# Gate operands in pairs of two tokens, and a low half that is kept unscaled

## The chip, the cores and the metric

The kernel runs on one core of a Trainium2 chip. The metric is the device time of one execution in microseconds. The engines are named as in the profile: PE (TensorE's matmuls), PEld (TensorE's weight loads), DVE (VectorE), ACT (ScalarE), POOL (GpSimd) and SP (SyncE, which issues the weight DMAs).

## The reference

A decoder trunk of two layers on 256 tokens with 1024 features. Each layer has a token-mixing part (a recurrent group, a state-space group and windowed attention behind one input and one output projection), a normalisation, and a retrieval part (PEER), which is the one that matters here:

```
q = (x @ wq)  ->  8 heads, two halves;  scores against 2 x 128 keys
top 16 of each half, top 16 of their sums  ->  16 expert pairs (i, j) per head
gate = softmax(best 16)
act  = gelu(x . u[i*128 + j]);   out = sum gate * act * v[i*128 + j]
```

So each token uses 8 x 16 = 128 of the 128 x 128 experts, with a gate for each.

## The kernel before, in words

The retrieval doesn't gather. It computes the activation of all 16384 experts for all 256 tokens (the first product), multiplies by a dense gate matrix that is zero but at the chosen experts, and multiplies the result by all rows of v (the second product).

*First product* (L987 to L993). 128 steps per layer, one per block of 128 experts. A weight block of 128 x 1024 f32 (512 KB) comes by DMA from SP into `raw`. It is split into a high part `hi` (ACT, L117) and a low part `lo` = raw - hi (L118; on DVE, and for every third block from the fourth to the 109th on POOL). 24 matmuls of 256 columns follow: hi with the high part of x, hi with its low part, and lo with the high part. After two steps `uevac` (L973 to L981) applies the gelu on ACT. Where the gates of a token are there already it multiplies by them (DVE, L978).

*Gates.* `routing` (L852 to L928) finds the chosen experts of 128 tokens: top-16 searches on DVE, one-hot work and matmuls against an identity in bf16 (L918, 16 matmuls in a row). It leaves, for every token, the two key indices of its 128 choices in `ijT` and the gates in `gT`, choices along the partitions. `gT` holds a high half float (scaled by GS = 2^15) and the rest as a second half float (scaled by LS = 2^11 more). `wgen` (L961 to L971) then goes through the 64 groups of four tokens in three stages: `gates` makes the operands on DVE, `wmm` the matmuls on PE, `apply` puts the result into `act`.

For a group, `gates` (L933 to L943) compares the indices with 0 to 127 (`eq`, L937: one-hot rows of both halves), multiplies the first one-hot by the two halves of the gate (`ga`, parts 0 and 1, L940), and makes a copy of the second one-hot divided by LS (`ga`, part 2, L942), which takes the low half's scale out again. All three have the four tokens innermost:

```
eq = pool.tile([128, 2, 128, TG], F16, name="eq", bufs=2)
A = pool.tile([128, 3, 128, TG], F16, name="ga", bufs=2)
```

`wmm` (L945 to L950) contracts over the 128 choices, for each token two matmuls of 128 x 128 x 128: high half with one-hot, low half with scaled one-hot. Both operands of a token are read with a step of four half floats. `apply` (L952 to L960) multiplies by 1 / GS into `act`: on DVE for the c experts whose activation is there (L956), on ACT as a plain copy for the others (L958). As the steps go on c grows, and so do L956 and L978.

*Order.* `wgen` is background work: one stage is issued per step of the first product, behind the routing of both token blocks. The instruction order on each engine is planned ahead of time from estimated costs and priorities, so an engine may do work ahead of its place in the source; each engine then runs its own list in order.

*Second product* (L995 to L1037). The two first pairs of `act` are split into the places of `eq` and `ga` (`early`, L997).

Of the kernel before, what the change touches and what calls it, by code (L numbers as in the profile page):

```python
# [8 lines left out]
F32R = mybir.dt.float32r  # L9
BF16 = mybir.dt.bfloat16  # L10
F16 = mybir.dt.float16
U32 = mybir.dt.uint32
AF = mybir.ActivationFunctionType
OP = mybir.AluOpType
AX = mybir.AxisListType

D = 1024
SEQ = 256
# [28 lines left out]
def trunk(ctx, tc, x, wst, ut, vr, pp_d, rb_d, lnrow, bd_d, keys_d, out):  # L47
    nc = tc.nc
    PE, ACT, DVE, POOL, SP = nc.tensor, nc.scalar, nc.vector, nc.gpsimd, nc.sync

    const = ctx.enter_context(tc.tile_pool(name="const", bufs=1))
    hpool = ctx.enter_context(tc.tile_pool(name="hpool", bufs=1))
    stream = ctx.enter_context(tc.tile_pool(name="stream", bufs=1))
    psum = ctx.enter_context(tc.tile_pool(name="psum", bufs=1, space=bass.MemoryType.PSUM))
    dram = ctx.enter_context(tc.tile_pool(name="dram", bufs=1, space=bass.MemoryType.DRAM))

# [1 line left out]
    items = []  # L58
    index = {}

# [79 lines left out]
        pump_dma()  # L140


# [1 line left out]
    mixp = tc.tile_pool(name="mix0", bufs=1)  # L144
    mix = mixp.__enter__()
    jp = mix.tile([128, 128], F32, name="jp")
    POOL.iota(jp, pattern=[[1, 128]], base=0, channel_multiplier=-1, allow_small_or_imprecise_dtypes=True)
    ident = const.tile([128, 128], F32, name="ident")
    POOL.tensor_scalar(ident, jp, 0.0, None, op0=OP.is_equal)
    iota4 = const.tile([128, 128, 4], F16, name="iota4")  # L150
    iota16 = const.tile([128, 16, 16], BF16, name="iota16")
    identb = const.tile([128, 128], BF16, name="identb")
    tri_le = const.tile([128, 128], F32, name="tri_le")
# [14 lines left out]
        return rb[:, l, o:o + w]  # L168

    def make_consts():  # L170
        POOL.iota(iota4, pattern=[[1, 128], [0, 4]], base=0, channel_multiplier=0, allow_small_or_imprecise_dtypes=True)
        POOL.iota(iota16, pattern=[[1, 16], [0, 16]], base=0, channel_multiplier=0, allow_small_or_imprecise_dtypes=True)
        POOL.tensor_scalar(identb, jp, 0.0, None, op0=OP.is_equal)
        POOL.tensor_scalar(tri_le, jp, 0.0, None, op0=OP.is_ge)
        POOL.tensor_scalar(tri_gt, jp, 0.0, None, op0=OP.is_lt)
        POOL.tensor_scalar(tri_gr, jp, 0.0, None, op0=OP.is_lt)
        for i in range(4):
            POOL.tensor_scalar(mask0[:, i, :], jp, 0.0, NEG, op0=OP.is_gt, op1=OP.mult)
        for i in range(2):
            POOL.tensor_scalar(mask1[:, i, 0, :], jp, 0.0, NEG, op0=OP.is_le, op1=OP.mult)  # L180
            POOL.tensor_scalar(mask1[:, i, 1, :], jp, 0.0, NEG, op0=OP.is_gt, op1=OP.mult)
# [10 lines left out]
    def mm(ps, lhsT, rhs, start, stop):  # L192
        PE.matmul(ps, lhsT, rhs, start=start, stop=stop)  # L193
# [4 lines left out]
    def acc_bank():  # L198
        return psum.tile([128, 512], F32, name="acc", bufs=4)

# [1 line left out]
    def layer_norm(h, pool, pre, gb, store, nxt=None, final=False, after=None):  # L202
        """h [128, 2, D] in place, stored to store; returns the transposed split operands."""
        ring = isinstance(gb[0], tuple)
        g, b = (rawtile(k) for k in gb) if ring else gb
        with tc.high_priority():
            hT = layer_norm_(h, pool, pre, g, b, store, nxt and index[nxt], final, after)
        for k in gb if ring else ():
            rawdone(k)
        return hT  # L210
# [93 lines left out]
    def seq(t):  # L304
        return [(w[0],) + tuple(int(ch) for ch in w[1:]) for w in t.split()]

    # (step, token block, part): r residual and sums, m mean and squares, v variance, n reciprocal root, s centre and
    # gain, o scale and bias with the transposes, l low halves, p the next weight pieces
    LN_ORDER = (
        seq("r00 r01 m0 v0 s00 s01 n00 r10 n01 r11 n02 m1 n03 v1 o00 o01 s10 n10 s11 n11 l00 n12 p1 n13 o10 o11 l01 l10 l11 p2"),  # L310
        seq("r00 r01 m0 s00 s01 v0 r10 n00 r11 n01 m1 n02 n03 o00 v1 o01 s10 n10 s11 n11 n12 n13 p1 o10 o11 l00 l01 l10 l11 p2"),
        seq("r00 r01 m0 s00 s01 v0 n00 n01 n02 r10 n03 r11 m1 s10 s11 v1 o00 n10 o01 n11 n12 n13 o10 o11"))

# [1 line left out]
    class Background:  # L315
        def __init__(self):
            self.q = []
# [39 lines left out]
        return y  # L357

    def log1p_exp_neg_abs(pool, o, xin, n, tag):
        """o = max(x, 0) + log1p(exp(-|x|)) on [128, n]"""  # L360
        a = pool.tile([128, n], F32, name=tag + "_a")
        e = pool.tile([128, n], F32, name=tag + "_e")
        q = pool.tile([128, n], F32, name=tag + "_q")
        ACT.activation(a, xin, AF.Abs)
        ACT.activation(e, a, AF.Exp, scale=-1.0)
        DVE.tensor_scalar(a, e, 2.0, None, op0=OP.add)
        DVE.reciprocal(a, a)
        DVE.tensor_tensor(e, e, a, op=OP.mult)
        DVE.tensor_tensor(a, e, e, op=OP.mult)
        DVE.tensor_scalar(q, a, 1.0 / 17.0, None, op0=OP.mult)  # L370
        for c in (15, 13, 11, 9, 7, 5, 3):
            DVE.scalar_tensor_tensor(q, q, 1.0 / c, a, op0=OP.add, op1=OP.mult)
        DVE.scalar_tensor_tensor(q, q, 1.0, e, op0=OP.add, op1=OP.mult)
        DVE.tensor_scalar(o, xin, 0.0, None, op0=OP.max)
        DVE.scalar_tensor_tensor(o, q, 2.0, o, op0=OP.mult, op1=OP.add)

# [1 line left out]
    def layer_consts(l, mix):  # L378
        av = mix.tile([128, 16], F32, name="av")
        sp4 = mix.tile([128, 4], F32, name="sp4")  # L380
# [12 lines left out]
    def mixer(l, mix, h, hT, pre):  # L393
# [3 lines left out]
        yTl = mix.tile([128, 16, SEQ], F32R, name="yTl")  # L397
        xs = mix.tile([128, N_XBC, SEQ], F32, name="xs")

        # small per-layer values  # L400
        dt = mix.tile([128, 2, 16], F32, name="dt")
        da = mix.tile([128, 2, 16], F32, name="da")
        das = mix.tile([128, 2, 2, 16], F32R, name="das")
# [25 lines left out]
            yield  # L429
            yield  # L430

        # causal depthwise convolution
        def conv(o, xp, w0, bias=None):
            if bias is None:
                DVE.tensor_scalar(o, xp[:, 0:SEQ], w0(0), None, op0=OP.mult)
# [287 lines left out]
                stages[st_](*units[u])  # L723
                yield

        # projection schedule
        order = [8, 9, 10, 11, 0, 1, 2, 3, 4, 5, 6, 7]
        for n, blk in enumerate(order):
            ps = bank([128, SEQ])
# [5 lines left out]
            if n == 3:  # L735
                ps = bank([128, SEQ])
# [8 lines left out]
        for blk in range(4):  # L745
            ps = bank([128, SEQ])
# [6 lines left out]
        for blk in range(4):  # L753
            ps = bank([128, SEQ])
# [5 lines left out]
        for i in range(6):  # L760
            ps = bank([128, SEQ])
# [7 lines left out]
        for nh in range(2):  # L769
            pz = [acc_bank() for _ in range(2)]  # L770
            for kp in range(4):
                hi, lo = weights(("w", l, n0 + nh * 4 + kp))
                for kk in range(2):
                    k = kp * 2 + kk
# [9 lines left out]
                ACT.activation(sz[:, tb, nh * 512:(nh + 1) * 512], pz[tb], AF.Silu)  # L784
        n0 += N_Z
        bg.add(ssm_final())
        # output projection
        po = [[acc_bank() for _ in range(2)] for _ in range(2)]
        oorder = list(range(0, 16))
        def out_mm(i, kb, w, tb):  # L790
# [26 lines left out]

    RA, RB2, RX = 2, 2, 1

# [1 line left out]
    def peer(l, pool, hT):  # L821
        hTh, hTl = hT
        act = pool.tile([128, 128, SEQ], F32, name="act")
        ijT = pool.tile([128, 2, SEQ], F16, name="ijT")
        gT = pool.tile([128, 2, SEQ], F16, name="gT")

        def view(slot, n):
            return act[:, slot:slot + n, :].rearrange("p a b -> p (a b)")
# [23 lines left out]
        def routing(tb):  # L852
            base = 92
# [48 lines left out]
            DVE.reciprocal(sm[:, 8:16], sm[:, 0:8])  # L902
            DVE.tensor_tensor(ex, ex, sm[:, 8:16, None].to_broadcast([128, 8, 16]), op=OP.mult)
            yield
            ts = slice(tb * 128, (tb + 1) * 128)
            for i in range(2):
                ACT.activation(tx, tf[:, :, i, :, None].to_broadcast([128, 8, 16, 16]).rearrange("p h a k -> p a h k"),
                               AF.Copy)
                DVE.tensor_tensor(oh.rearrange("p a (h k) -> p a h k", k=16),
                                  pab[:, i, None, :].to_broadcast([128, 16, 128]).rearrange("p a (h k) -> p a h k", k=16),  # L910
                                  iota16[:, :, None, :].to_broadcast([128, 16, 8, 16]), op=OP.is_equal)
                yield
                DVE.tensor_tensor(oh, oh, tx.rearrange("p a h k -> p a (h k)"), op=OP.mult)
                for _ in range(3):
                    yield
                ps = bank([128, 128])
                for a in range(16):
                    mm(ps, oh[:, a, :], identb, a == 0, a == 15)  # L918
                ACT.activation(ijT[:, i, ts], ps, AF.Copy)
                yield  # L920
            ps = bank([128, 128])
            PE.transpose(ps, ex.rearrange("p h k -> p (h k)"), ident)
            yield
            ACT.activation(gT[:, 0, ts], ps, AF.Copy, scale=GS)
            DVE.scalar_tensor_tensor(gr, ps, GS, gT[:, 0, ts], op0=OP.mult, op1=OP.subtract)
            ACT.activation(gT[:, 1, ts], gr, AF.Copy, scale=LS)
            yield

        state = dict(c=0, t=0)
        TG = 4  # L930
        GS, LS = float(2 ** 15), float(2 ** 11)

        def gates(t0):  # L933
            eq = pool.tile([128, 2, 128, TG], F16, name="eq", bufs=2)
            A = pool.tile([128, 3, 128, TG], F16, name="ga", bufs=2)
            sh = [128, 2, 128, TG]
            DVE.tensor_tensor(eq, iota4[:, None, :, :].to_broadcast(sh),  # L937
                              ijT[:, :, None, t0:t0 + TG].to_broadcast(sh), op=OP.is_equal)
            # gate = (hi + lo / LS) / GS in half floats
            DVE.tensor_tensor(A[:, 0:2], eq[:, 0:1].to_broadcast(sh), gT[:, :, None, t0:t0 + TG].to_broadcast(sh),  # L940
                              op=OP.mult)
            DVE.tensor_scalar(A[:, 2], eq[:, 1], 1.0 / LS, None, op0=OP.mult)  # L942
            return A, eq  # L943

        def wmm(A, eq):  # L945
            ps = bank([128, TG, 128])
            for i in range(TG):
                mm(ps[:, i, :], A[:, 0, :, i], eq[:, 1, :, i], True, False)
                mm(ps[:, i, :], A[:, 1, :, i], A[:, 2, :, i], False, True)
            return ps  # L950

        def apply(t0, ps):  # L952
# [34 lines left out]
        for jp_ in range(64):  # L987
            ps = psum.tile([128, 2, SEQ], F32, name="acc", bufs=4)
            for i in range(2):
# [2 lines left out]
            uevac(jp_, ps)  # L992
        bg.drain()  # L993

        # second product  # L995
        po = [[acc_bank() for _ in range(2)] for _ in range(2)]
        early = [[pool.tile([128, w], F32R, name=nm, bufs=2)[:, 0:2 * SEQ] for _ in range(2)]  # L997
                 for nm, w in (("eq", 512), ("ga", 768))]
        ring = []

        def gslot(jp_):
# [34 lines left out]
                v_mm(j, w, tb)  # L1036
        return po  # L1037

# [1 line left out]
    h = mix.tile([128, 2, D], F32, name="h")  # L1040
    gb = mix.tile([128, 2, D], F32, name="y")
    for i in range(2):
# [107 lines left out]
```

## Time and profile before

| | us |
|---|---|
| median of 3 runs | 2103.95 (2101.63 to 2104.25) |
| span of the profiled execution | 2106.6 |
| PE busy in it | 2030.2 (96%) |
| DVE busy | 1548.2 (73%) |
| ACT busy | 1062.8 (50%) |
| POOL busy | 238.3 (11%) |

The time of the profiled execution outside its span isn't shown. Matmuls are pipelined: the profile gives each a duration of some 0.3 us, while the next one starts much earlier, so the pace of matmuls is read from the chain of waits, which merges a run of them into one piece, and not from their durations. VectorE's instructions overlap a little too: the start of the next one says what one costs. PE's clock was granted in full in almost the whole span.

### The profile page before, as it was taken

What the parts mean: (1) busy time and instruction counts of PE and PEld (TensorE: products, weight loads), DVE (VectorE), ACT (ScalarE), POOL (GpSimd) and SP (SyncE); (2) the same over time, 40 slices, a digit from 0 to 9 for tenths busy, and PEclk for the clock granted to TensorE, in tenths of its full rate; (3) what the DMA queues carried; (4) which work ended last, traced back from release to release, by engine and by line L of the source; (5) the groups of instructions that cost most, each with busy time, mean ns of one, the idle gap of its engine ahead of it and who ended that gap; (6) DMA issues with size and microseconds to landing.
All of it is one profiled execution on the core that took longest, in us unless ns stands there. A gap on an engine that the chain in (4) does not pass through costs nothing. (4 is left out here: it accounts for less than half of the span.)

```text
span 2106.6 us, 33808 instructions
## 1 busy us (share of the span) xinstructions
PE 2030.2 (96%) x13212; PEld 1835.5 (87%) x13212; DVE 1548.2 (73%) x2713; ACT 1062.8 (50%) x1523; POOL 238.3 (11%) x120
## 2 busy tenths in 40 slices
PE   7999889999999999999989999899999999999998
PEld 6887889999999888888888769899999998888886
DVE  8786697379999655555687867963999995555555
ACT  5576455454443544444566755554444344444444
POOL 3100122222220000000010001222222200000000
PEclk9999999999999999999999999999999999999999
DMA  6434445544434666666654335455444446666665
GB/s 206 136 110 150 152 152 168 180 141 140 132 130 135 195 194 194 192 194 195 197 180 139 108 133 170 155 173 174 140 132 134 136 151 190 193 196 192 195 195 170
DMA packets 95919, 344.84 MB, mean 164 GB/s; under 512 B 11680, under 2 KB 11952, under 8 KB 95760
## 3 DMA queue, kind: packets, MB, share of 16 engines
q1 hardware_dynamic: 95552, 342.27, 50.3%
q8 instruction: 103, 1.69, 0.3%
q0 software_dynamic: 208, 0.42, 0.1%
q14 instruction: 56, 0.46, 0.1%
HBM read 339.51 MB, written 3.15 MB: 163 GB/s over the span
## 5 line engine op out<-in xcount | busy, mean ns | idle before, releaser
L118 DVE TENSOR_TENSOR lo<-raw,hi 128x1024 fp32r<-128x1024 f32 x544 | 677.5, 1246 | 383.9 <-ACT hi L117 383.5
L117 ACT ACTIVATE hi<-raw 128x1024 fp32r<-128x1024 f32 x630 | 663.8, 1056 | 452.2 <-PE acc L193 342.5
L193 PE MATMUL acc<-hTh,lo 128*128 128x256 f32 x2048 | 581.8, 284 | 20.1 <-DVE lo L118 18.8
L193 PE MATMUL acc<-hTh,hi 128*128 128x256 f32 x2048 | 592.0, 289 | 0.2 <-ACT hi L117 0.2
L193 PE MATMUL acc<-hTl,hi 128*128 128x256 f32 x2048 | 580.1, 283 | 0.0
L193 PEld LDWEIGHTS acc<-hTh,lo 128*128 128x128 f32 x2048 | 392.1, 191 | 24.3 <-DVE lo L118 22.4
L193 PE MATMUL acc<-hi,hTl 128*128 128x512 f32 x1056 | 411.4, 390 | 0.0
L193 PE MATMUL acc<-hi,hTh 128*128 128x512 f32 x1056 | 411.2, 390 | 0.0
L193 PE MATMUL acc<-lo,hTh 128*128 128x512 f32 x1056 | 411.1, 389 | 0.0
L193 PEld LDWEIGHTS acc<-hTh,hi 128*128 128x128 f32 x2048 | 394.3, 193 | 0.7 <-ACT hi L117 0.4
L193 PEld LDWEIGHTS acc<-hTl,hi 128*128 128x128 f32 x2048 | 392.8, 192 | 0.1
L118 POOL TENSOR_TENSOR lo<-raw,hi 128x1024 fp32r<-128x1024 f32 x86 | 223.6, 2602 | 1046.7 <-ACT hi L117 1015.7
L193 PEld LDWEIGHTS acc<-hi,hTh 128*128 128x128 f32 x1056 | 198.3, 188 | 41.6 <-issue 0.7
L193 PEld LDWEIGHTS acc<-hi,hTl 128*128 128x128 f32 x1056 | 198.2, 188 | 41.1
L193 PEld LDWEIGHTS acc<-lo,hTh 128*128 128x128 f32 x1056 | 198.3, 188 | 41.1
L193 PE MATMUL w<-hTh,hi 128*128 128x256 f32 x560 | 161.4, 299 | 7.5 <-DVE y L495 5.7
L1011 ACT ACTIVATE hTh<-act 128x512 fp32r<-128x512 f32 x124 | 77.7, 631 | 166.2 <-PE acc L193 166.2
L1012 DVE TENSOR_TENSOR hTl<-act,hTh 128x512 fp32r<-128x512 f32 x124 | 85.4, 693 | 97.4 <-ACT hTh L1011 97.4
L193 PE MATMUL w<-hTh,lo 128*128 128x256 f32 x560 | 156.9, 289 | 0.0
L193 PE MATMUL w<-hTl,hi 128*128 128x256 f32 x560 | 155.4, 287 | 0.0
L958 ACT ACTIVATE act<-w 128x272 f32<-128x272 f32 (+32 forms) x128 | 61.1, 478 | 146.5 <-DVE act L956 145.8
L193 PE MATMUL w<-eq,ga 128*128 128x128 f16 x512 | 128.0, 294 | 6.9 <-DVE ga L940 6.9
(268 smaller groups left out, 2323.5 us busy)
## 6 DMA issues: line engine op xcount, KB each, us to landing
raw<-in_ut SPq DMA_DIRECT2D x256, 512.0 KB, 3.5
raw<-in_vr SPq DMA_DIRECT2D x256, 512.0 KB, 3.5
raw<-in_wst SPq DMA_DIRECT2D x118, 512.0 KB, 3.5
raw<-in_lnrow SPq DMA_DIRECT2D x8, 512.0 KB, 3.6
hd<-h SPq DMA_DIRECT2D x4, 512.0 KB, 3.9
raw<-hd SPq DMA_DIRECT2D x4, 512.0 KB, 3.5
h<-in_x SPq DMA_DIRECT2D x2, 512.0 KB, 5.7
y<-in_lnrow SPq DMA_DIRECT2D x2, 512.0 KB, 7.0
```

What stands on the lines that cost most here:

```text
L117: ACT.activation(hi, raw, AF.Copy)
L118: (POOL if n in on_pool else DVE).tensor_tensor(lo, raw, hi.bitcast(F32), op=OP.subtract)
L193: PE.matmul(ps, lhsT, rhs, start=start, stop=stop)
L958: ACT.activation(v[:, :, c:128], ps[:, :, c:128], AF.Copy, scale=1.0 / GS)
L1011: ACT.activation(gh, src, AF.Copy)
L1012: DVE.tensor_tensor(gl, src, gh.bitcast(F32), op=OP.subtract)
```

## The change

The four tokens of a group are stored as two pairs: the innermost dimension of `eq` and `ga` is two tokens, outside it come the 128 keys, outside that the two pairs. `iota` shrinks with them. `ijT` and `gT` are stored by group, so that four half floats of one index or one gate half lie side by side, and are read as pairs. The low half of the gate is no longer multiplied by LS. The scaled copy of the second one-hot (part 2 of `ga`) is dropped, and both matmuls of a token use the same one-hot. `ga` and its reuse in `early` become smaller. Comments are removed.

```diff
-    iota4 = const.tile([128, 128, 4], F16, name="iota4")
+    iota2 = const.tile([128, 128, 2], F16, name="iota2")
...
-        POOL.iota(iota4, pattern=[[1, 128], [0, 4]], base=0, channel_multiplier=0, allow_small_or_imprecise_dtypes=True)
+        POOL.iota(iota2, pattern=[[1, 128], [0, 2]], base=0, channel_multiplier=0, allow_small_or_imprecise_dtypes=True)
...
-        ijT = pool.tile([128, 2, SEQ], F16, name="ijT")
-        gT = pool.tile([128, 2, SEQ], F16, name="gT")
+        TG = 4
+        ijT = pool.tile([128, SEQ // TG, 2, TG], F16, name="ijT")
+        gT = pool.tile([128, SEQ // TG, 2, TG], F16, name="gT")
...
-            ts = slice(tb * 128, (tb + 1) * 128)
+            gs = slice(tb * 128 // TG, (tb + 1) * 128 // TG)
+            grp = lambda ap: ap.rearrange("p (g t) -> p g t", t=TG)
...
-                ACT.activation(ijT[:, i, ts], ps, AF.Copy)
+                ACT.activation(ijT[:, gs, i, :], grp(ps), AF.Copy)
...
-            ACT.activation(gT[:, 0, ts], ps, AF.Copy, scale=GS)
-            DVE.scalar_tensor_tensor(gr, ps, GS, gT[:, 0, ts], op0=OP.mult, op1=OP.subtract)
-            ACT.activation(gT[:, 1, ts], gr, AF.Copy, scale=LS)
+            ACT.activation(gT[:, gs, 0, :], grp(ps), AF.Copy, scale=GS)
+            DVE.scalar_tensor_tensor(grp(gr), grp(ps), GS, gT[:, gs, 0, :], op0=OP.mult, op1=OP.subtract)
+            ACT.activation(gT[:, gs, 1, :], grp(gr), AF.Copy)
...
         def gates(t0):
-            eq = pool.tile([128, 2, 128, TG], F16, name="eq", bufs=2)
-            A = pool.tile([128, 3, 128, TG], F16, name="ga", bufs=2)
-            sh = [128, 2, 128, TG]
-            DVE.tensor_tensor(eq, iota4[:, None, :, :].to_broadcast(sh),
-                              ijT[:, :, None, t0:t0 + TG].to_broadcast(sh), op=OP.is_equal)
-            # gate = (hi + lo / LS) / GS in half floats
-            DVE.tensor_tensor(A[:, 0:2], eq[:, 0:1].to_broadcast(sh), gT[:, :, None, t0:t0 + TG].to_broadcast(sh),
-                              op=OP.mult)
-            DVE.tensor_scalar(A[:, 2], eq[:, 1], 1.0 / LS, None, op0=OP.mult)
+            g = t0 // TG
+            eq = pool.tile([128, 2, TG // 2, 128, 2], F16, name="eq", bufs=2)
+            A = pool.tile([128, 2, TG // 2, 128, 2], F16, name="ga", bufs=2)
+            sh = [128, TG, 128, 2]
+            def pairs(ap):
+                return ap.rearrange("p c (a e) -> p (c a) e", e=2)[:, :, None, :].to_broadcast(sh)
+            DVE.tensor_tensor(eq.rearrange("p c a k e -> p (c a) k e"), iota2[:, None, :, :].to_broadcast(sh),
+                              pairs(ijT[:, g]), op=OP.is_equal)
+            DVE.tensor_tensor(A.rearrange("p c a k e -> p c (a k) e"),
+                              eq[:, 0].rearrange("p a k e -> p (a k) e")[:, None].to_broadcast([128, 2, TG * 64, 2]),
+                              pairs(gT[:, g]), op=OP.mult)
             return A, eq
...
             for i in range(TG):
-                mm(ps[:, i, :], A[:, 0, :, i], eq[:, 1, :, i], True, False)
-                mm(ps[:, i, :], A[:, 1, :, i], A[:, 2, :, i], False, True)
+                for c in range(2):
+                    mm(ps[:, i, :], A[:, c, i // 2, :, i % 2], eq[:, 1, i // 2, :, i % 2], c == 0, c == 1)
...
-        early = [[pool.tile([128, w], F32R, name=nm, bufs=2)[:, 0:2 * SEQ] for _ in range(2)]
-                 for nm, w in (("eq", 512), ("ga", 768))]
+        early = [[pool.tile([128, w], F32R, name=nm, bufs=2) for _ in range(2)]
+                 for nm, w in (("eq", 512), ("ga", 512))]
```

## Rows read from the trace of the kernel before

**Rows 1.** The page: busy time of the engines, and DVE's tenths in 40 slices.
```profile
PE 2030.2 (96%) x13212; PEld 1835.5 (87%) x13212; DVE 1548.2 (73%) x2713; ACT 1062.8 (50%) x1523; POOL 238.3 (11%) x120
...
DVE  8786697379999655555687867963999995555555
```

**Rows 2.** Windows of the gate stretches: length, busy time (instructions) per engine, clock, DMA.
```profile
442.00:545.00 103.00, 103.00 (x864) 101.57 (x864) 96.64 (x138) 49.81 (x80) 24.24 (x9) 1.00 0.42 137
545.00:686.00 141.00, 137.26 (x1137) 133.92 (x1136) 137.43 (x182) 58.26 (x110) 21.57 (x8) 1.00 0.41 133
1478.00:1580.00 102.00, 102.00 (x856) 100.55 (x855) 93.36 (x134) 50.05 (x79) 24.62 (x9) 1.00 0.41 134
1580.00:1722.00 142.00, 138.86 (x1153) 135.63 (x1152) 139.91 (x187) 57.48 (x107) 24.74 (x9) 1.00 0.41 134
```

**Rows 3.** The late windows, instructions of the first product's banks alone: PE, PEld, DVE, ACT.
```profile
545.00:686.00 141.00, 111.73 (x865) 106.22 (x864) 9.67 (x18) 14.64 (x36) 1.00 0.41 133
...
1580.00:1722.00 142.00, 112.18 (x865) 106.34 (x864) 9.21 (x18) 14.77 (x36) 1.00 0.41 134
```

**Rows 4.** The chain of waits, layer 1: start us, us, what.
```profile
1454.60 0.91 PE w L193 x16
...
1485.36 0.95 PE w L193 x8
1486.31 2.88 PE acc L193 x24
...
1752.04 344.81 PE acc L193 x1520
```

**Rows 5.** Timeline: weight loads of the routing's matmuls (bf16) and of a gate group.
```profile
1454.44 0.90 PEld L193 LDWEIGHTS <-act 128*128 128x128 bf16 x16
...
1481.37 0.82 PEld L193 LDWEIGHTS <-ga 128*128 128x128 f16 x8
```

**Rows 6.** Timeline: a POOL split beside DVE, and a late step on DVE.
```profile
458.48 2.71 POOL L118 TENSOR_TENSOR lo<-raw,hi 128x1024 fp32r<-128x1024 f32 x1 [7.92 <-ACT hi L117]
...
459.03 2.71 DVE L940 TENSOR_TENSOR ga<-eq,gT 128x1024 f16<-128x1024 f16 x1
...
649.97 0.71 DVE L937 TENSOR_TENSOR eq<-iota,ijT 128x1024 f16<-128x1024 f16 x1
650.57 1.24 DVE L118 TENSOR_TENSOR lo<-raw,hi 128x1024 fp32r<-128x1024 f32 x1
651.71 0.63 DVE L978 TENSOR_TENSOR act<-act,acc 128x440 f32<-128x440 f32 x1
652.23 0.71 DVE L940 TENSOR_TENSOR ga<-eq,gT 128x1024 f16<-128x1024 f16 x1
652.83 0.32 DVE L942 TENSOR_SCALAR ga<-eq 128x512 f16<-128x512 f16 x1
653.03 1.21 DVE L956 SCALAR_TENSOR_TENSOR act<-w,act 128x440 f32<-128x440 f32 x1
654.12 0.71 DVE L937 TENSOR_TENSOR eq<-iota,ijT 128x1024 f16<-128x1024 f16 x1
```

**Rows 7.** Instructions that write eq and ga: duration ns min/median/max, first and last start.
```profile
L937 DVE TENSOR_TENSOR eq<-iota,ijT x128: 671/683/2859, 349.7 to 1716.0; 128x1024 f16<-128x1024 f16 x128
L940 DVE TENSOR_TENSOR ga<-eq,gT x128: 671/684/2883, 351.1 to 1718.3; 128x1024 f16<-128x1024 f16 x128
L942 DVE TENSOR_SCALAR ga<-eq x128: 231/282/325, 352.9 to 1718.9; 128x512 f16<-128x512 f16 x128
```

**Rows 8.** Groups of DVE by shape: busy us, mean ns of one, idle before.
```profile
L519 DVE TENSOR_TENSOR sr<-tri_le,das 128x512 fp32r<-128x512 f32 x32 | 21.1, 684 | 1.1 <-PE w L193 1.0
...
L956 DVE SCALAR_TENSOR_TENSOR act<-w,act 128x464 f32<-128x464 f32 x4 | 5.0, 1248 | 0.0
...
L956 DVE SCALAR_TENSOR_TENSOR act<-w,act 128x224 f32<-128x224 f32 x4 | 2.7, 668 | 0.9 <-ACT act L980 0.9
```

**Rows 9.** The ACT instructions that write ijT and gT's low half: duration min/median/max.
```profile
L919 ACT ACTIVATE ijT<-w x8: 265/269/278, 329.0 to 1465.5; 128x128 f16<-128x128 f32 x8
...
L926 ACT ACTIVATE gT<-act x4: 309/310/310, 346.4 to 1469.6; 128x128 f16<-128x128 f32 x4
```

More of the change, by code (lines that the diff above doesn't have):

```diff
@@ L923, in routing @@
             yield
-            ACT.activation(gT[:, 0, ts], ps, AF.Copy, scale=GS)
-            DVE.scalar_tensor_tensor(gr, ps, GS, gT[:, 0, ts], op0=OP.mult, op1=OP.subtract)
-            ACT.activation(gT[:, 1, ts], gr, AF.Copy, scale=LS)
+            ACT.activation(gT[:, gs, 0, :], grp(ps), AF.Copy, scale=GS)
+            DVE.scalar_tensor_tensor(grp(gr), grp(ps), GS, gT[:, gs, 0, :], op0=OP.mult, op1=OP.subtract)
+            ACT.activation(gT[:, gs, 1, :], grp(gr), AF.Copy)
             yield
         state = dict(c=0, t=0)
-        TG = 4
-        GS, LS = float(2 ** 15), float(2 ** 11)
+        GS = float(2 ** 15)
         def gates(t0):
-            eq = pool.tile([128, 2, 128, TG], F16, name="eq", bufs=2)
-            A = pool.tile([128, 3, 128, TG], F16, name="ga", bufs=2)
-            sh = [128, 2, 128, TG]
-            DVE.tensor_tensor(eq, iota4[:, None, :, :].to_broadcast(sh),
-                              ijT[:, :, None, t0:t0 + TG].to_broadcast(sh), op=OP.is_equal)
-            DVE.tensor_tensor(A[:, 0:2], eq[:, 0:1].to_broadcast(sh), gT[:, :, None, t0:t0 + TG].to_broadcast(sh),
-                              op=OP.mult)
-            DVE.tensor_scalar(A[:, 2], eq[:, 1], 1.0 / LS, None, op0=OP.mult)
+            g = t0 // TG
[9 more added lines that the diff above has]
+                              pairs(gT[:, g]), op=OP.mult)
             return A, eq
```

## The prediction, made before the changed kernel ran

> **What bounds the kernel now.** I read the page first. TensorE is busy for 96% of the span and VectorE for 73%, but VectorE's line of tenths is uneven: in two places, one in each layer, it stands at 8 or 9 for a run of slices [rows 1]. A share of the whole span can't tell what the change is worth there, so the windows view of those places came second. It separates each place into two stretches: an early one in which TensorE has no idle time at all and VectorE is at 91 to 94%, and a late one in which VectorE is at 97 to 99% and TensorE now has gaps [rows 2]. In both, every step of the first product (one block of 128 experts, 24 matmuls) carries one gate group of four tokens (8 matmuls in half floats, and eq, ga and its third part on VectorE).
>
> Steps: the early stretch of layer 0 has 864 matmuls, or 864 / 32 = 27 steps in 103 us, 3.815 us each; layer 1 has 856 / 32 = 26.75 steps in 102 us, 3.813 each [rows 2]. The chain of waits gives the same from the other side: 24 matmuls take 2.88 us and the 8 of a gate group 0.95 [rows 4], together 3.83. So the early step is TensorE's own work and nothing else. VectorE's work in it is 96.64 / 27 = 3.58 us (layer 0) and 93.36 / 26.75 = 3.49 (layer 1): close behind. The late stretches hold 865 / 24 = 36 steps each, 141 / 36 = 3.92 and 142 / 36 = 3.94 us; the other 272 and 288 matmuls are 34 and 36 gate groups [rows 2, 3]. There VectorE binds: its own work is 137.43 / 36 = 3.82 and 139.91 / 36 = 3.89 [rows 2], and the timeline shows its instructions end to end [rows 6].
>
> **The change part by part.**
>
> *The third part of ga goes.* 128 instructions of 0.282 us median [rows 7]. The duration is not what VectorE gets back, since instructions overlap at their ends: in the timeline L942 starts at 652.83 and the next instruction at 653.03, 0.20 us later [rows 6]. I take 0.205 us per group. In the late stretch it lies on the path: 34 x 0.205 = 7.0 us in layer 0, 36 x 0.205 = 7.4 in layer 1. In the early stretch it only lowers VectorE's work, to 3.375 and 3.285 us a step, and is worth something only if TensorE gets faster too.
>
> *The gate matmuls step by 4 bytes instead of 8.* Their number and shape stay; both operands are now read with every second half float. Eight take 0.95 us, 119 ns each; the 16 matmuls of the same 128 x 128 shape on gapless bf16 take 0.91 us, 57 ns each, just beside them in the chain [rows 4], and the weight loads keep the same two paces (16 in 0.90 us, 8 in 0.82) [rows 5]. So the step costs something now. No row has a 4-byte step in half floats; the ends are 57 ns (as gapless) and 119 ns (no change; a loss is left out, since a shorter step touches no more memory). To choose, I use the f32 matmuls, whose neighbouring columns are 4 bytes apart: 256 columns take 2.88 / 24 = 120 ns, 512 columns take 344.81 / 1520 = 227 ns [rows 4]. The slope is 107 / 256 = 0.42 ns per column with 13 ns besides. The gate matmul at 8 bytes is (119 - 13) / 128 = 0.83 per column, just twice that: it behaves as if time went with the bytes passed over. At 4 bytes it would be 128 x 0.42 + 13 = 67 ns at most, 57 at best. I take 62: eight take 0.50 us, and TensorE's step becomes 2.88 + 0.50 = 3.38 us.
>
> [...]
>
> *eq and ga in pairs of two tokens.* Each still has 1024 results per partition, and runs of the small operand shrink from four half floats (8 bytes) to two (4 bytes), repeated 128 times. Now they take 683 and 684 ns median [rows 7], 0.60 from start to start [rows 6]: two results per tick. The nearest row is L519: an f32 word read again 128 times against another SBUF operand, 512 elements in 684 ns [rows 8], as fast per word as eq is now. So reading the same 4-byte word again costs nothing, and I take no change. A gain is left out, since 512 ticks in 0.68 us is the rate of L519 too. The upper ends: one result per tick, as L118 (1024 elements, 1.13 us from start to start [rows 6]), +0.53 us each; and L956, whose elements lie a KB apart, at (1248 - 668) / 240 = 2.42 ns each [rows 8]: 512 such ticks take 1.24 us, +0.64 each. I keep the first as the end that the rivals use, as eq would reach it by falling to the rate of another row of its own kind of instruction.
>
> [...]
>
> *The rest costs nothing.* The new order of ijT and gT makes eight ACT writes (0.269 us) and four of the low half (0.310) [rows 9] land in runs of four half floats; they lie in the routing, ahead of the gate stretch, beside TensorE's and VectorE's work. Doubled, with nothing to cover them, they would be 8 x 0.27 + 4 x 0.31 = 3.4 us over both layers. The half-size iota is one instruction at the start. No DMA, queue or wait is added; eq and ga are still freed by the group's last matmul, and ga is complete 0.2 us sooner.
>
> *What is late next, and the sum.* Early: TensorE needs 3.38 us, VectorE 3.375 (layer 0) and 3.285 (layer 1). With two engines level, I add what VectorE still idles per step where it binds today, (141 - 137.43) / 36 = 0.10 us [rows 2]: 3.46 and 3.45. Saved: 27 x 0.355 + 26.75 x 0.363 = 19.3 us. Late: 14.4 us, as TensorE's 3.38 is now well below VectorE's 3.82 - 0.19 = 3.63 and 3.89 - 0.205 = 3.69. GpSimd's share stays: while it splits a weight (2.71 us), a VectorE instruction with two SBUF operands is held as long [rows 6], and that stall counts in VectorE's work before and after. Sum 33.7 us. The profiled execution has a span of 2106.6 us, 0.13% above the median of the runs, 2103.95; its time around the span isn't shown, and I take it as nothing. 2106.6 - 33.7 = 2072.9, and against the median 2070.
>
> **The rivals.**
>
> *TensorE gains nothing:* the cost sits in half floats whose neighbours are not adjacent, and any such step is read at 119 ns. Early nothing is saved. Late, VectorE's 137.4 - 7.0 = 130.4 us would be below TensorE's 36 x 2.88 + 34 x 0.95 = 136, so of 141 us at most 5 go, and in layer 1 at most 4; with gaps some 7 together: 2097. [...] For it: no row at a 4-byte step. Against: the factor of two between 0.42 and 0.83.
>
> *VectorE pays for the shorter runs: slower.* If eq and ga fall to one result per tick, VectorE has 2 x 0.53 - 0.205 = +0.855 us a group: late 70 x 0.855 = 60; early 3.54 + 0.855 + 0.10 = 4.50 against 3.815, 53.75 x 0.68 = 37. Together +97: 2201. The point from which it decides: with p us more for each instruction, late costs 70 x (2p - 0.205) and early 53.75 x (2p - 0.38); the sum is zero at p = 0.14, so from about 0.82 us for eq and ga the kernel is slower. [...] For it: no row with pairs of half floats. Against: L519.
>
> *Other order.* Each engine's order is planned from estimated costs, which change; a later weight split or a GpSimd split that meets VectorE more often (2 us each, 35 splits in the four stretches) can give or take some 8 us.
>
> **How the numbers follow.** The forecast 0.64: 2061, if the two engines add no waits to each other (54 x 0.43 + 14.4 + the late idle, 5.7), to 2081, if a gate matmul takes 85 ns (a step of 3.61: 54 x 0.20 + 12); TensorE unchanged 0.16 (2093 to 2101); VectorE slower 0.14 (2108 to 2201); the planned order 0.06. The range, 2054 to 2101, holds the first two, with the 8 us of the order below them and what it can of it above. About 0.2% (4 us) is what a measurement of this kernel tells from no change: faster 0.78, same 0.08 (the worse end of TensorE unchanged, and a mild VectorE penalty), slower 0.14.
>
> **What would show it.** Right: the group's 8 matmuls at 0.46 to 0.54 us in the chain, eq and ga at 0.68 median, no L942 row, early steps of 3.4 to 3.5 us with both engines over 95%, late steps of 3.7 with VectorE at 97% and more TensorE idle than now. Wrong: 8 matmuls still at 0.95, or eq or ga above 0.82. A gate matmul between 67 and 119 ns would leave the forecast's direction and spoil its early half.

## The result

The changed kernel takes 2075.6 us (median of 4 runs) against 2104.1 for the kernel before: ratio 0.9858, 95% interval 0.9839 to 0.9878. Forecast was 2070, 33.7 us less; measured are 28.5 between the medians and 34.2 between the two profiled spans (2106.6 and 2072.4).

The chain of waits of the kernel after, layer 1 (start us, us, what), answers to [rows 4]:

```profile
1454.87 0.48 PE w L193 x8
1455.34 2.92 PE acc L193 x24
1458.27 0.48 PE w L193 x8
...
1487.95 0.69 DVE ga L947
1488.64 0.63 DVE act L963
1489.27 0.59 DVE eq L945
```

Eight gate matmuls take 0.48 us, 60 ns each, where they took 0.95. At 1485.36 us, after nine such steps, the chain leaves TensorE and goes on through ACT and VectorE; before, it stayed on TensorE there. The instructions on eq and ga of the kernel after (duration ns min/median/max, first and last start us) answer to [rows 7]; L945, L947 and L1018 are what L937, L940 and L1011 were:

```profile
L193 PE MATMUL w<-eq,ga x1024: 217/218/233, 427.1 to 1685.7; 128*128 128x128 f16 x171
L945 DVE TENSOR_TENSOR eq<-iota,ijT x128: 671/682/2790, 345.7 to 1682.3; 128x1024 f16<-128x1024 f16 x128
L947 DVE TENSOR_TENSOR ga<-eq,gT x128: 636/685/2890, 347.1 to 1684.6; 128x1024 f16<-128x1024 f16 x128
L1018 ACT ACTIVATE eq<-act x2: 624/624/624, 665.2 to 1692.3; 128x512 fp32r<-128x512 f32 x2
```

The medians of eq and ga are those of before: pairs cost VectorE nothing. The same view of the kernel before gives the marks for an account by place:

```profile
L193 PE MATMUL w<-eq,ga x512: 282/296/301, 430.4 to 1719.8; 128*128 128x128 f16 x171
L1011 ACT ACTIVATE eq<-act x2: 622/624/625, 684.9 to 1727.3; 128x512 fp32r<-128x512 f32 x2
```

The first gate matmul of layer 0 starts 3.3 us earlier (430.4, 427.1), the first split for the second product 19.7 us earlier (684.9, 665.2): the gate stretch of layer 0 gave 16.4. In layer 1 the first gate group starts 19.0 us earlier (1473.88 in the chain of before, 1454.87 in that of after) and the split 35.0 (1727.3, 1692.3): 16.0. So 32.4 us come from the two stretches. The 3.3 us ahead of the first arise where both kernels do the same work, and go with the execution rather than with the change: e8 below, an edit of the kernel before, has its first gate matmul at 426.9, and e1 and e3, edits of the kernel after, at 430.1 and 430.5.

The windows of the kernel after (length, busy time and instructions of PE, PEld, DVE, ACT, POOL; clock; DMA) stand against [rows 2]; the second fence gives the same windows for instructions of the first product's banks alone (PE, PEld, DVE, ACT), 24 matmuls a step:

```profile
437.00:531.00 94.00, 91.23 (x853) 88.97 (x852) 86.83 (x110) 48.53 (x79) 22.15 (x9) 1.00 0.45 145
531.00:666.00 135.00, 124.69 (x1143) 120.42 (x1143) 131.77 (x149) 58.81 (x110) 24.50 (x9) 1.00 0.43 142
1459.00:1553.00 94.00, 91.09 (x849) 89.03 (x848) 85.64 (x106) 48.12 (x79) 23.97 (x9) 1.00 0.44 145
1553.00:1692.00 139.00, 129.15 (x1188) 124.78 (x1187) 135.77 (x157) 60.60 (x113) 25.75 (x9) 1.00 0.43 141
```

```profile
437.00:531.00 94.00, 82.48 (x637) 77.61 (x636) 3.50 (x13) 10.97 (x26) 1.00 0.45 145
531.00:666.00 135.00, 112.24 (x871) 106.12 (x871) 9.53 (x18) 14.87 (x36) 1.00 0.43 142
1459.00:1553.00 94.00, 82.79 (x641) 78.10 (x640) 3.29 (x13) 10.95 (x26) 1.00 0.44 145
1553.00:1692.00 139.00, 116.12 (x900) 109.64 (x899) 9.91 (x19) 15.74 (x38) 1.00 0.43 141
```

These are 26.5, 36.3, 26.7 and 37.5 steps: 3.54 and 3.52 us early (3.815 before), 3.72 and 3.71 late (3.92 and 3.94 before). TensorE has gaps everywhere now, and VectorE is at 91 to 92% early and at 98% late.

### The profile page after: what moved, and what is told of

Its sections match the earlier page's. It is cut to its first block, busy times and chain, and to the rows that moved or that the text cites. A ratio compares the mean times of both kernels' runs of the same rounds, so it can differ in the third digit from the quotient of the medians.

```text
span 2072.4 us, 33596 instructions
## 1 busy us (share of the span) xinstructions
PE 1977.5 (95%) x13212; PEld 1778.9 (86%) x13212; DVE 1517.2 (73%) x2585; ACT 1060.6 (51%) x1523; POOL 239.2 (12%) x120
## 5 line engine op out<-in xcount | busy, mean ns | idle before, releaser
L118 DVE TENSOR_TENSOR lo<-raw,hi 128x1024 fp32r<-128x1024 f32 x544 | 680.0, 1250 | 381.9 <-ACT hi L117 380.9
L118 POOL TENSOR_TENSOR lo<-raw,hi 128x1024 fp32r<-128x1024 f32 x86 | 223.8, 2605 | 1016.1 <-ACT hi L117 797.4
L1018 ACT ACTIVATE hTh<-act 128x512 fp32r<-128x512 f32 x124 | 77.7, 631 | 166.1 <-PE acc L193 166.1
L963 DVE SCALAR_TENSOR_TENSOR act<-w,act 128x240 f32<-128x240 f32 (+32 forms) x128 | 121.8, 953 | 9.5 <-ACT act L987 9.5
```

The costliest lines, as they stand in the source:

```text
L118: (POOL if n in on_pool else DVE).tensor_tensor(lo, raw, hi.bitcast(F32), op=OP.subtract)
L963: DVE.scalar_tensor_tensor(v[:, :, 0:c], ps[:, :, 0:c], 1.0 / GS, v[:, :, 0:c], op0=OP.mult, op1=OP.mult)
L1018: ACT.activation(gh, src, AF.Copy)
```

## The experiments

**Each half of the change alone.** First the pairs with the scaled third copy kept (e1), then the old layout without the third copy (e2).

```diff
 e1, against the kernel after
-            A = pool.tile([128, 2, TG // 2, 128, 2], F16, name="ga", bufs=2)
+            A = pool.tile([128, 3, TG // 2, 128, 2], F16, name="ga", bufs=2)
...
+            DVE.tensor_scalar(A[:, 2], eq[:, 1], 1.0 / LS, None, op0=OP.mult)
...
+                    oh2 = A[:, 2] if c else eq[:, 1]
 e2, against the kernel before
-            A = pool.tile([128, 3, 128, TG], F16, name="ga", bufs=2)
+            A = pool.tile([128, 2, 128, TG], F16, name="ga", bufs=2)
...
-            DVE.tensor_scalar(A[:, 2], eq[:, 1], 1.0 / LS, None, op0=OP.mult)
...
-                mm(ps[:, i, :], A[:, 1, :, i], A[:, 2, :, i], False, True)
+                mm(ps[:, i, :], A[:, 1, :, i], eq[:, 1, :, i], False, True)
```

> The change without its second half: operands in pairs of two tokens, but the low half still scaled and the scaled third copy of the one-hot rows still made. Theory (each half relieves one of two engines that are nearly level; VectorE binds as soon as TensorE is relieved): the 8 gate matmuls take 0.48 us, but VectorE keeps its 3.58 and 3.49 us per step early and 3.82 and 3.89 late, so early steps fall only to about 3.65 and late ones not at all: some 9 us faster than before, ratio 0.996. Rival A (the gain is TensorE's pace alone, the dropped copy is hidden): all of the change's 28 us, ratio 0.987. Rival B (the gain is the dropped copy alone): no difference, ratio 1.000.

> The change without its first half: four tokens innermost as before, low half unscaled, third copy dropped. Theory: the 8 gate matmuls stay at 0.95 us, so early steps stay at 3.82 (TensorE); late steps can fall from 3.92 to TensorE's 3.83 only: 5 to 7 us faster, ratio 0.997. Rival A (TensorE's pace alone): no difference. Rival B (the dropped copy alone): 128 x 0.205 = 26 us faster, ratio 0.987. If the two halves simply add, this run and the run with the third copy kept give together the change's 28 us; by the theory they give together only about 15.

> The changed kernel once more, beside the others on one chip: ratio 0.984 to 0.988, 8 gate matmuls at 0.48 us, eq and ga at 0.68 us median. By every theory the same; it is the yardstick for the others.

On one chip, where the kernel before takes 2104.2 us: e1 2096.1, ratio 0.9954 (0.9937 to 0.9971); e2 2096.0, ratio 0.9968 (0.9954 to 0.9982); both together, the kernel after again, 2076.9, ratio 0.9866 (0.9843 to 0.9888). By the medians the halves give 8 us each, 16 together, and both at once 27; by the ratios 9.7 and 6.7, again 16 together, and both at once 28. The windows show what stopped each. Windows of e1 in layer 0:

```profile
440.00:540.00 100.00, 94.62 (x869) 91.26 (x867) 93.40 (x137) 50.10 (x82) 27.04 (x9) 1.00 0.40 138
540.00:680.00 140.00, 127.77 (x1144) 121.63 (x1145) 136.49 (x184) 58.02 (x109) 23.21 (x8) 1.00 0.39 136
```

Windows of e2 in layer 0:

```profile
440.00:540.00 100.00, 100.00 (x839) 98.58 (x839) 90.32 (x111) 49.60 (x80) 24.81 (x9) 1.00 0.40 137
540.00:675.00 135.00, 135.00 (x1132) 133.15 (x1131) 131.38 (x149) 60.00 (x108) 21.27 (x8) 1.00 0.40 141
```

In e1 VectorE is at 97% late while TensorE idles; early neither is full (TensorE 95%, VectorE 93%), with steps of about 3.68 us. In e2 TensorE is without a gap in both windows. Both rivals, one engine alone, are out: neither half gives the whole, and the sum of the halves falls 11 us short of both at once.

**Which operand's step costs TensorE.** The kernel after, with the moving operand (the one-hot rows, e3) or the stationary one (the gates, e4) read with a step of 8 bytes. Both form another gate matrix, so they stand for their timing alone; each ran once.

```diff
 e3
-                    mm(ps[:, i, :], A[:, c, i // 2, :, i % 2], eq[:, 1, i // 2, :, i % 2], c == 0, c == 1)
+                    rows = eq[:, 1].rearrange("p a k e -> p (a k e)").rearrange("p (k t) -> p k t", t=TG)
+                    mm(ps[:, i, :], A[:, c, i // 2, :, i % 2], rows[:, :, i], c == 0, c == 1)
 e4
-                    mm(ps[:, i, :], A[:, c, i // 2, :, i % 2], eq[:, 1, i // 2, :, i % 2], c == 0, c == 1)
+                    cols = A[:, c].rearrange("p a k e -> p (a k e)").rearrange("p (k t) -> p k t", t=TG)
+                    mm(ps[:, i, :], cols[:, :, i], eq[:, 1, i // 2, :, i % 2], c == 0, c == 1)
```

> The changed kernel, but the gate matmuls read the moving operand (one-hot rows) with a step of 8 bytes and the stationary operand (gates) with 4, as before the change and after it; the rows so read are not those of one token, so the gate matrix is a different one. All VectorE work is as in the changed kernel. Theory (the time of a gate matmul goes with the bytes the moving operand passes over, 0.42 ns per 4 bytes): 8 matmuls at 0.95 us, early steps back to 3.83. Rival (it is the weight load that the stride slowed): 8 matmuls at 0.48 us, time as the changed kernel.

> The other way round: stationary operand (gates) read with a step of 8 bytes, moving operand (one-hot rows) with 4; again the gate matrix is a different one and VectorE's work that of the changed kernel. Theory (moving operand): 8 matmuls stay at 0.48 us. Rival (weight load): 8 matmuls at 0.95 us. If each is slow by itself at 8 bytes, both runs show 0.95.

The chain of e3, layer 1:

```profile
1469.61 0.93 PE w L193 x8
1470.55 2.87 PE acc L193 x24
```

The chain of e4, layer 1:

```profile
1460.52 0.51 PE w L193 x8
1461.03 2.92 PE acc L193 x24
```

It is the moving operand: at 8 bytes it gives back the old pace, 117 ns, and 2099.5 us, while the stationary operand at 8 bytes costs 0.03 us per group, 3 to 4 ns a matmul, and leaves 2077.9. VectorE, ACT and PE have the same lists of instructions, in the same order, in e3, e4 and the kernel after.

**One token innermost instead of two (e5).** This takes the step of both matmul operands down to 2 bytes and the small operand's run on VectorE to one half float.

```diff
-            eq = pool.tile([128, 2, TG // 2, 128, 2], F16, name="eq", bufs=2)
-            A = pool.tile([128, 2, TG // 2, 128, 2], F16, name="ga", bufs=2)
-            sh = [128, TG, 128, 2]
+            eq = pool.tile([128, 2, TG, 128], F16, name="eq", bufs=2)
+            A = pool.tile([128, 2, TG, 128], F16, name="ga", bufs=2)
+            sh = [128, 2 * TG, 128]
...
-                    mm(ps[:, i, :], A[:, c, i // 2, :, i % 2], eq[:, 1, i // 2, :, i % 2], c == 0, c == 1)
+                    mm(ps[:, i, :], A[:, c, i, :], eq[:, 1, i, :], c == 0, c == 1)
```

> The changed kernel with one token innermost instead of two: eq and ga hold 128 gapless half floats per token, the small operand of eq and ga is one half float read 128 times. Theory: the 8 matmuls gain almost nothing more (0.45 us against 0.48, as the routing's gapless 57 ns), but VectorE falls to one result per tick: eq and ga 1.15 to 1.25 us median instead of 0.68, +1.1 us per group, so some 60 to 110 us slower than before, ratio 1.03 to 1.05. Rival (a repeated value costs nothing, as L519 shows for f32): eq and ga stay at 0.68 and the time is that of the changed kernel or 1 to 3 us better.

Measured: 2175 us (two runs, 2169 and 2180), ratio 1.0335 (1.0299 to 1.0372). The instructions on eq and ga in e5:

```profile
L945 DVE TENSOR_TENSOR eq<-iota,ijT x128: 1167/1211/2848, 345.4 to 1779.7; 128x1024 f16<-128x1024 f16 x128
L947 DVE TENSOR_TENSOR ga<-eq,gT x128: 1205/1218/3314, 346.7 to 1781.9; 128x1024 f16<-128x1024 f16 x128
```

This is the price that the slower rival of the prediction put on pairs, +0.53 us an instruction, and it is real one step further: with one half float read again the 1024 results take 1.21 us, with a pair read again 0.68. (VectorE's order of instructions in e5 is another one too, so the price is read from the durations and not from the 2175 us.) TensorE gets nothing more for it. The gate group in the chain of e5, layer 1:

```profile
1502.34 0.48 PE w L193 x8
```

That is 0.48 us, not the 0.45 I had expected. So two tokens are the one choice of these three at which neither engine pays.

**GpSimd's splits out of the gate stretches, in the kernel after (e6) and in the kernel before (e8).** VectorE takes over the 38 splits.

```diff
-        on_pool.update(index["u", l, j] for j in range(4, 110, 3))
+        on_pool.update(index["u", l, j] for j in range(4, 53, 3))
```

> The changed kernel, but GpSimd splits weight blocks only up to the 52nd of each first product, ahead of the gates; the 19 later splits per layer go to VectorE. Theory (VectorE binds in the gate stretches, and a GpSimd split holds one of its instructions for about 2 us, while the same split on VectorE costs it 1.13): VectorE wins some 0.6 to 0.9 us per split, 38 splits, so 20 to 30 us less VectorE work, of which early steps can use only what lies above TensorE's 3.40: 12 to 20 us faster than the changed kernel, ratio to before 0.977 to 0.981; no eq or ga above 0.75 us in the gate stretches. Rival (the hold is time in which VectorE would have waited anyway, or the split on GpSimd is worth its price): 38 x 1.13 = 43 us more VectorE work, some 20 to 40 us slower than the changed kernel, ratio 0.995 to 1.005.

> The kernel before with GpSimd's weight splits ending at the 52nd block, ahead of the gates, and nothing of the change. The theory that the change gives what the less relieved engine lets through: early TensorE holds the step at 3.82, so nothing there; late VectorE falls below TensorE's 3.83, so steps from 3.93 to about 3.84, 72 steps: 6 to 8 us faster than before, ratio 0.996 to 0.997, although the same edit gave the changed kernel 27 us. Rival (the hold by GpSimd is worth the same in both kernels): 27 us faster, ratio 0.987.

e6: 2050.1 us, ratio 0.9745 (0.9730 to 0.9761), 26.8 us below the kernel after on the same chip, and so the fastest of all; more than the 12 to 20 expected. e8: 2096.4 us, ratio 0.9964 (0.9951 to 0.9977). The same edit is worth 27 us in one kernel and 8 in the other. Windows of e6 in layer 0:

```profile
435.00:525.00 90.00, 90.00 (x847) 88.88 (x847) 85.76 (x119) 49.36 (x79) 0.00 (x0) 1.00 0.45 154
525.00:645.00 120.00, 118.85 (x1116) 116.77 (x1115) 119.88 (x153) 57.13 (x103) 0.00 (x0) 1.00 0.43 150
```

Windows of e8 in layer 0:

```profile
440.00:540.00 100.00, 100.00 (x839) 98.58 (x838) 90.11 (x145) 49.20 (x80) 0.00 (x0) 1.00 0.39 138
540.00:675.00 135.00, 135.00 (x1132) 133.14 (x1131) 131.60 (x189) 61.41 (x108) 0.00 (x0) 1.00 0.39 137
```

e8 ends on the same wall as e2: TensorE without a gap, 839 and 1132 matmuls in the same 100 and 135 us, whichever way VectorE was relieved. In e6 TensorE is full early, at 847 / 32 = 26.5 steps in 90 us, 3.40 us each: the step that its own work sets, which the change alone had not reached. Late, 836 matmuls of the first product, or 34.8 steps, take 120 us: 3.45 each against 3.72 in the kernel after, with VectorE at 100%. There lies most of the gain. The instructions on eq and ga in e6 show what had been in the way:

```profile
L945 DVE TENSOR_TENSOR eq<-iota,ijT x128: 671/691/708, 345.3 to 1650.2; 128x1024 f16<-128x1024 f16 x128
L947 DVE TENSOR_TENSOR ga<-eq,gT x128: 634/682/702, 346.7 to 1652.5; 128x1024 f16<-128x1024 f16 x128
```

The longest is 0.71 us, where the kernel after had 2.8 and 2.9. In its trace 36 of these 256 instructions last longer than 0.75 us, 2.34 on average, and each of the 36 overlaps a split on GpSimd: they were held by it. By what in it, no run shows.

Other idle time comes and goes with these splits. VectorE's own split in the early window of layer 0 (busy us, mean ns, idle time before it), for the kernels before (442:545) and after (437:531) and for e6 (435:525), with the `eq` row of e6 and TensorE's only wait in the kernel after (us, times, longest):

```profile
L118 DVE TENSOR_TENSOR lo<-raw,hi 128x1024 fp32r<-128x1024 f32 x18 | 21.9, 1216 | 5.0 <-ACT hi L117 5.0
L118 DVE TENSOR_TENSOR lo<-raw,hi 128x1024 fp32r<-128x1024 f32 x18 | 21.9, 1218 | 5.0 <-ACT hi L117 5.0
L118 DVE TENSOR_TENSOR lo<-raw,hi 128x1024 fp32r<-128x1024 f32 x27 | 32.9, 1220 | 0.0
L945 DVE TENSOR_TENSOR eq<-iota,ijT 128x1024 f16<-128x1024 f16 x26 | 18.0, 692 | 4.1 <-PE w L193 3.5
PE w L193 <- DVE ga L947: 2.6, 5, 1.0
```

With GpSimd's splits VectorE idles 5.0 us for ACT's high part, before the change as after it; without them not at all, and what idle time is left waits for TensorE. TensorE waits for `ga` alone, in the other three windows too, and never for a split of GpSimd's, so a low part that comes late from there is not what lengthened the step.

## Why the prediction was right, point by point

- *Which engine binds where.* Right. The early stretch was TensorE's and the late one VectorE's: e2, which relieves VectorE alone, leaves the early step where it was, and e1, which relieves TensorE alone, stops at VectorE late. One of the signs named ahead did not come: VectorE early is at 91 to 92%, not over 95%.
- *The gate matmuls.* Taken 62 ns, measured 60; TensorE's step 3.38, measured 0.48 + 2.92 = 3.40. The reasoning by bytes passed over gave a sound bound, but it is no general rule: at 2 bytes, in e5, the eight take 0.48 us as at 4. No row of the kernel before separated the step from the type; e3 does: with type, layout and VectorE's work unchanged, a moving step of 8 bytes alone brings back 117 ns. The rival that nothing is gained on TensorE fell with the 60 ns.
- *eq and ga in pairs.* Taken as unchanged, measured 682 and 685 ns against 683 and 684. L519 was the right row. The ticks of the forecast stand for rates of rows, 1024 results in 0.60 us from start to start for `eq` and in 1.13 for L118; no row shows a tick itself.
- *The third copy.* Taken as 14.4 us late. Late steps fell to 3.72 and 3.71 us where the working gives 3.73, so 36 x 0.20 + 36 x 0.23 = 15.5 us.
- *The early sum: the term that was mis-sized.* Steps of 3.46 and 3.45 were forecast, 3.54 and 3.52 measured: 27 x 0.275 + 26.75 x 0.293 = 15.3 us in place of 19.3. Part of that is arithmetic: TensorE's 3.38 and the allowance of 0.10 make 3.48, not 3.46 and 3.45, which is 1.3 us of saving too many. The rest is the allowance itself. VectorE's work came out lower than forecast (86.83 / 26.5 = 3.28, and 85.64 / 26.7 = 3.21; why, I did not follow), but it idles (94 - 86.83) / 26.5 = 0.27 and 0.31 us a step. I took 0.10 from the stretch where VectorE binds alone.
- *Where the allowance stood.* [rows 2] had the early figure: (103 - 96.64) / 27 = 0.24 and (102 - 93.36) / 26.75 = 0.32, and 5.0 of the 6.4 us in layer 0 wait for ACT's high part and not for TensorE, so a faster TensorE could not be counted on to fill it. (With it the working gives steps of 3.61, 0.07 and 0.09 too much, as VectorE's work came out lower.) Two engines do not idle by being level alone: in e6's late window VectorE is busy for 119.88 and TensorE for 118.85 of 120 us. With GpSimd's splits away the wait for ACT is gone and the early step is 3.40, though VectorE's work per step is hardly less (85.76 / 26.5 = 3.24). In e8's early window no split of VectorE's waits for ACT either. So the idle time goes when GpSimd's splits go; the planned order moves with them, and the path from a hold to ACT's late high part I did not follow.
- *GpSimd's share* I counted as the same before and after. Its time was, but not its price: moving the splits is worth 8 us with TensorE at 119 ns a gate matmul, and 27 at 60. The two SBUF operands of the forecast are those of the one instruction in [rows 6], and not shown as a condition: in the kernel after, L435, which reads one tensor and a weight per partition, takes 2.50 us beside a split (from 1083.38) against a median of 0.35, while L963, which reads the gate matmuls' result, takes 0.70 beside one (from 443.93) and 0.71 ahead of it.
- *The planned order.* The traces settle most of it. VectorE and ACT run one and the same list in the kernel before and in e1, and one and the same in e2, e3 and the kernel after; GpSimd's differs by the size of `iota` alone, and PE's list is the same before and after. So the new layout is compared with the old at one order on either side, 8 us (before to e1) and 19 (e2 to the kernel after). Among these kernels the order changes with the dropped copy alone: beside the 128 copies, 12 of VectorE's 2585 instructions and 4 of ACT's 1476 have moved, and their share of e2's 8 us was not measured.
- *The upper end.* The 2081 counts a step of 3.61 for a gate matmul of 85 ns; 2.88 + 8 x 0.085 is 3.56. Nothing hangs on it, as the measured 60 ns lies below.

Between the medians the gain is 28.5 us, with 26 to 34 by the interval of the ratio; the 32.4 us of the traced stretches lie within it.

## What to carry to other kernels

Where two engines are nearly level, as here, two small edits that relieve one each can be worth more together (27 us) than the sum of their own measurements (16), and an edit that was tried alone and gave little (e2 and e8, 8 us each) is worth trying again after the other engine has been relieved (the same edits then gave 19 and 27). Read the layout of an operand from both engines that touch it: here four tokens innermost cost TensorE a factor of two (0.95 against 0.48 us per 8 gate matmuls), one token costs VectorE nearly a factor of two (1211 against 682 ns for `eq`), and two tokens cost neither. A share of work on a slow helper engine has to be priced by what it holds up (some 1.7 us on average here, 2.34 against 0.68, and the waits that follow) and not only by what it takes over (1.13 us). The idle time of an engine that is second in a stretch is read from that stretch, with what it waits for.

## What the runs showed of the hardware that I had not expected

- The step of the stationary operand hardly matters: 0.51 us per 8 gate matmuls at 8 bytes against 0.48 at 4, while the moving operand's takes them to 0.93.
- Between 4 and 2 bytes the step makes no difference: 0.48 us per 8 in the kernel after and in e5, where both operands are gapless.
- A single half float read again and again nearly doubles the time of the instruction on `eq` (1211 against 682 ns median for 1024 results); a pair of them doesn't (682 against 683 with four), and a single f32 word read again takes 684 ns for 512 results [rows 8].
- A split on GpSimd holds one instruction on `eq` or `ga` by 1.7 us on average, and in the early windows of layer 0 VectorE's 5.0 us of waiting for ACT come and go with GpSimd's splits (before and after against e6).
